# Issuing the plain copies of the weight sums on SyncE's DMA queue instead of GpSimd's

## The chip, the core and the metric

The kernel runs on one core of a Trainium2 chip. The metric is the device time of one execution in microseconds. An execution is one launch that reads all inputs from device DRAM and leaves the output there.

## What is computed

The reference is one layer of a decoder on 1024 tokens of width 1024, with 16 learned tokens put in front (T = 1040):

```
h   = concat([meta, x])                                  # (1040, 1024)
u   = rmsnorm(h, norm_mix_g)
x_lru, g_lru, v_cc, g_cc = split(u @ w_in, 4)            # 512 columns each
xc  = causal_conv(x_lru, width 4)
y_lru = rg_lru(xc) * gelu(g_lru)                         # gates, then a linear recurrence over time
c   = causal_conv(v_cc * sigmoid(g_cc), width 31)
y_cc  = silu(layernorm(c))
h   = h + concat([rmsnorm(y_lru), rmsnorm(y_cc)]) @ w_out
m   = rmsnorm(h, norm_mlp_g) @ w_mlp_up                  # 1024 -> 4096
h   = h + square(relu(m)) @ w_mlp_down                   # 4096 -> 1024
out = rmsnorm(h, norm_final_g)[16:]                      # float32
```

## The kernel before

Every large matrix product is made of three products on TensorE (PE): each float32 operand is split into a rounded part "hi" and the rest "lo", and hi*hi, hi*lo and lo*hi are added up in PSUM. A weight therefore goes through three steps: a DMA of 512 KB brings a block of 128 x 1024 numbers to SBUF, ScalarE (ACT) casts it to hi (L313), and VectorE (DVE) subtracts to get lo (L322). This is `split_w` (L556).

The tokens are worked on in two halves of 512 (the first with the 16 learned tokens). In time, the kernel does: the projection with w_in, the two convolutions and the recurrence (until about 215 us); w_out for half A (until about 270 us); the MLP of half A in 16 groups of 256 hidden columns, beside which DVE does the long convolution of half B; w_out for half B (about 540 to 580 us); and from about 680 us the MLP of half B in 8 blocks q of 512 hidden columns, by `up_fast` and `down_fast`.

`up_fast` and `down_fast` use a product scheme for 2 x 2 blocks that needs 7 block products instead of 8. Four of the seven use sums and differences of weight blocks. These depend on the weights alone, so they are made ahead of time by DMAs, into DRAM tiles `ws_up_*` and `ws_down_*`: `weight_sums` (L623) yields eight DMAs for each block, four plain copies of a weight block into t[0] to t[3], and four DMAs that add onto such a tile (`accum_op` add, L418): y onto t[0], z onto t[2], then t[0] onto t[1], then t[1] onto t[3]. There are 15 such sets (8 of up, 7 of down), 60 copies and 60 adds of 512 KB each. `load_sum` (L1176) later loads a finished sum like any weight.

The order of all instructions is set by a planner. Each step is added with a duration, what it reads and what it writes (`Plan.add`, L136); `forward` (L166) plays the steps through, engine by engine, by priority, and the program is written out in the order in which that play starts them. Its engine "sp" is SyncE, which issues DMAs alone; "pool" is GpSimd, which issues DMAs and a little arithmetic. Both issue in program order, so that an instruction which waits holds up all behind it. SyncE carries the loads of x, of w_out, w_mlp_up, w_mlp_down and of the sums, and the stores of the output (L425). GpSimd carries part of the w_in loads, small parameters, and the DMAs of the sums (`dma_pool`, L417).

The sums are spread over the plan by `tick` (L641): after every 6 us of planned PE work, from 40 us on, one DMA of a set is added, with the lowest priority and "after" that PE step. This "after" is a rule of the plan alone. In the program there is a semaphore wait only where data or a buffer demands it, or where one of the eight semaphores that a queue's DMAs use in turn is still in use.

Of the kernel before, what the change touches and what calls it, by code (L numbers as in the profile page):

```python
# [274 lines left out]
def hymba_kernel(  # L275
# [16 lines left out]
    def refs(*a):  # L292
        return [r for r in a if isinstance(r, Ref)]

    def val(v):
        return v.ap() if isinstance(v, Ref) else v
# [108 lines left out]
    def dma(o, src, nbytes, q="sp", after=()):  # L405
        e = nc.sync if q == "sp" else nc.gpsimd
        return pl.add(q, 0.47 if q == "sp" else 1.02, lambda: e.dma_start(val(o), src), [], [o],
                      nbytes=nbytes, after=after)
# [8 lines left out]
    def dma_pool(o, src, nbytes, add=False, after=()):  # L417
        kw = {"accum_op": ALU.add} if add else {}  # L418
        if add and isinstance(src, Ref):
            kw["max_dma_last_dim"] = 1024  # L420
        return pl.add("pool", 1.02, lambda: nc.gpsimd.dma_start(val(o), val(src), **kw),  # L421
                      refs(src) + ([o] if add else []), [o], nbytes=nbytes, after=after)
# [200 lines left out]
    def weight_sums(q, kind):  # L623

        blk, k, (x, y, z, v) = ((up_block, k4, ((1, 0), (1, 1), (0, 0), (0, 1))) if kind == "up"
                                else (dn_block, k2, ((0, 1), (0, 0), (1, 1), (1, 0))))
        t = [pl.fixed(dr.tile([P, 1024], F32, name=f"ws_{kind}_{q}_{n}"))[:, 0:1024] for n in range(4)]
        n = 1 << 19
        for o, src in ((t[0], x), (t[1], z), (t[2], x), (t[3], v)):
            yield lambda after, o=o, src=src: dma_pool(o.view(k), blk(q, *src), n, after=after)  # L630
        yield lambda after: dma_pool(t[0].view(k), blk(q, *y), n, True, after)
        yield lambda after: dma_pool(t[2].view(k), blk(q, *z), n, True, after)
        yield lambda after: dma_pool(t[1], t[0], n, True, after)
        wsum[q, kind] = t
        yield lambda after: dma_pool(t[3], t[1], n, True, after)

    sums = [(q, kind) for q in range(NG // 2) for kind in ("up", "down")][:-1]

    pace = {"sums": (f for s in sums for f in weight_sums(*s)), "pe": 0.0, "next": SUM_FROM}

    def tick(op):  # L641
# [130 lines left out]
    for name, src in (("a", gate_a_w), ("x", gate_x_w)):  # L772
# [3 lines left out]
            lambda a, o=o: a.rearrange("p (c n) -> p c n", c=NCT)[:, :, o * 64:(o + 1) * 64]),  # L776
# [686 lines left out]
```

## Time and profile before

| | us |
|---|---|
| three runs | 1024.51, 1024.62, 1027.83 |
| median | 1024.62 |
| the profiled execution, device time | 1022.59 |
| its span, from the first to the last instruction | 1020.8 |
| PE busy within the span | 1002.9 |
| mean granted clock of PE, as a share of the full one | 0.993 |

The rows of the profile are read like this. A row of the waits names who waited, for whom, us in total, how often, and the longest. A row of the chain of waits has the start in us, the length in us, and what ran (or which DMA was in flight). A row of the timeline has start, length, engine, line, operation, what is written <- what is read, and in brackets how long the engine stood before it and what ended that. A row of the DMA issues has the transfer, the queue that issued it, how many, KB each, and the median time in us from issue to landing. A row of the table by stretch has the stretch, its length, then busy time and number of instructions of PE, PE's weight loads, DVE, ACT and GpSimd (POOL), the granted clock as a share, the busy share of the 16 DMA engines, and GB/s. Tiles w are weights in SBUF, s and c activations, mm, tr and cv PSUM banks, ws_up and ws_down sums in DRAM.

### The profile page before, as it was taken

To read this page: it belongs to the slowest core of one execution; us is meant where nothing else is said; L and a number is where in the kernel's file an instruction comes from. 1 tells how busy PE (TensorE), PEld (TensorE's weight loads), DVE (VectorE), ACT (ScalarE), POOL (GpSimd) and SP (SyncE) were. 2 spreads that over 40 slices of the span, in tenths; PEclk is the share of its full clock that TensorE was granted. 3 is DMA by queue.
4 is the path that set the end of the run, shared out by engine and by line. 5 is a ranking of instruction groups with operands and counts; after the bars stand their busy time and mean duration, and the time that the engine had idled before them with its cause. 6 is when DMAs were issued, how large, how long until landed. Compare 5 with 4: busy or idle time off the path is not lost.

```text
span 1020.8 us, 14830 instructions
## 1 busy us (share of the span) xinstructions
PE 1002.9 (98%) x5624; PEld 864.0 (85%) x5624; DVE 833.1 (82%) x1445; ACT 524.4 (51%) x824; POOL 151.7 (15%) x179
## 2 busy tenths in 40 slices
PE   9999999999999999999899999999999999999997
PEld 7888998988797888878778888889988988989985
DVE  6798898698989999999566575577998797897875
ACT  5831045656678333334353373357666656556644
POOL 4324324212200032222222200000000000000001
PEclk9999999999999999999899999999999999999999
DMA  9449999999922299999999952234856565566522
GB/s 310 101 89 229 194 209 206 212 262 247 225 86 82 83 245 275 243 242 218 246 274 269 212 145 83 97 112 143 282 186 191 177 196 186 177 195 189 183 103 83
DMA packets 113240, 191.19 MB, mean 187 GB/s; under 512 B 6668, under 2 KB 73244, under 8 KB 113168
## 3 DMA queue, kind: packets, MB, share of 16 engines
q0 software_dynamic: 50112, 76.39, 35.4%
q1 hardware_dynamic: 63056, 113.85, 34.1%
q8 instruction: 44, 0.72, 0.3%
q14 instruction: 28, 0.23, 0.1%
HBM read 186.02 MB, written 67.11 MB: 248 GB/s over the span
## 4 chain that ended last, share of the span: by engine, by line
PE 85%; DMA 5%; DVE 4%; ACT 3%; issue 1%; SPq 0%; ACTq 0%
PE mm L388 54%; PE mm L373 17%; PE cv L373 8%; PE tr L373 4%; ACT s L315 2%; DMA s<-in_x_dram 1%; DMA w<-in_w_mlp_down_dram 1%; DVE cv L327 1%; DMA w<-in_w_mlp_up_dram 1%; DVE s L322 1%; PE tr L401 1%; DVE w L322 1%; DMA w<-in_w_out_dram 1%; ACT w L313 1%; DMA w<-in_w_in_dram 1%
## 5 line engine op out<-in xcount | busy, mean ns | idle before, releaser
L388 PE MATMUL mm<-s,w 128*128 128x512 f32 (+2 forms) x2016 | 369.5, 343 | 2.3 <-ACT w L313 1.0
L388 PEld LDWEIGHTS mm<-s,w 128*128 128x128 f32 x2016 | 315.7, 189 | 49.0 <-ACT w L313 1.3
L388 PE MATMUL mm<-w,s 128*128 128x512 f32 (+1 forms) x1260 | 299.2, 395 | 4.3 <-DVE s L322 4.3
L313 ACT CAST w<-w 128x1024 fp32r<-128x1024 f32 x193 | 200.0, 1047 | 193.1 <-DMA w<-in_w_mlp_down_dram 62.0
L388 PEld LDWEIGHTS mm<-w,s 128*128 128x128 f32 x1260 | 235.0, 189 | 59.2 <-DVE s L322 5.8
L322 DVE TENSOR_TENSOR w<-w,w 128x1024 fp32r<-128x1024 f32 x193 | 234.9, 1220 | 55.1 <-ACT w L313 54.5
L327 DVE SCALAR_TENSOR_TENSOR cv<-c,prm,cv 128x512 f32<-128x512 f32 x232 | 162.5, 750 | 0.4
L373 PEld LDWEIGHTS mm<-s,w 128*128 128x128 f32 x1152 | 139.2, 188 | 1.4
L373 PE MATMUL mm<-s,w 128*128 128x256 f32 x1152 | 140.3, 281 | 0.0
L322 DVE TENSOR_TENSOR s<-s,s 128x512 fp32r<-128x512 f32 (+4 forms) x183 | 122.3, 686 | 18.0 <-ACT s L315 15.7
L322 DVE TENSOR_TENSOR s<-mm,s 128x512 f32<-128x512 f32 x144 | 97.6, 686 | 38.5 <-PE mm L388 17.8
L315 ACT ACTIVATE s<-s 128x512 f32<-128x512 f32 (+2 forms) x152 | 95.3, 632 | 33.6 <-DVE s L322 30.7
L373 PE MATMUL cv<-w,s 128*128 128x512 f32 x336 | 83.5, 394 | 0.0
L313 ACT CAST s<-s 128x512 fp32r<-128x512 f32 (+2 forms) x83 | 50.6, 622 | 57.8 <-DVE s L322 40.1
L373 PEld LDWEIGHTS cv<-w,s 128*128 128x128 f32 x336 | 62.2, 188 | 13.7
L322 POOL TENSOR_TENSOR s<-s,s 128x512 f32<-128x512 f32 x3 | 4.6, 1541 | 421.8 <-ACT s L315 421.8
L421 POOL DMA_DIRECT2D ws_up<-in_w_mlp_up_dram x48 | 48.5, 1279 | 47.3 <-DMA ws_up<-in_w_mlp_up_dram 47.3
L313 ACT COPY s<-mm 128x512 f32<-128x512 f32 (+2 forms) x48 | 24.4, 513 | 60.2 <-PE mm L373 32.1
L421 POOL DMA_DIRECT2D ws_down<-in_w_mlp_down_dram x42 | 39.6, 1251 | 56.8 <-DMA ws_down<-in_w_mlp_down_dram 56.8
L322 DVE TENSOR_TENSOR c<-mm,c 128x512 f32<-128x512 f32 (+2 forms) x49 | 31.0, 634 | 14.4 <-PE mm L388 14.0
L315 ACT ACTIVATE s<-mm 128x512 f32<-128x512 f32 x40 | 23.7, 594 | 34.0 <-PE mm L388 33.3
L373 PE MATMUL mm<-w,s 128*128 128x512 f32 x168 | 41.1, 393 | 0.0
(133 smaller groups left out, 718.3 us busy)
## 6 DMA issues: line engine op xcount, KB each, us to landing
w<-in_w_mlp_down_dram SPq DMA_DIRECT2D x57, 512.0 KB, 4.3
w<-in_w_mlp_up_dram SPq DMA_DIRECT2D x56, 512.0 KB, 4.8
ws_up<-in_w_mlp_up_dram POOLq DMA_DIRECT2D x48, 512.0 KB, 9.4
ws_down<-in_w_mlp_down_dram POOLq DMA_DIRECT2D x42, 512.0 KB, 9.4
w<-ws_up SPq DMA_DIRECT2D x32, 512.0 KB, 3.9
w<-ws_down SPq DMA_DIRECT2D x28, 512.0 KB, 4.0
w<-in_w_in_dram POOLq DMA_DIRECT2D x24, 512.0 KB, 8.4
ws_up<-ws_up POOLq DMA_DIRECT2D x16, 512.0 KB, 7.8
```

The lines of the kernel that those rows point to most:

```text
L313: nc.scalar.copy(val(o), val(i))
L315: nc.scalar.activation(out=val(o), in_=val(i), func=func, scale=val(scale), **kw)
L322: return pl.add(eng, dur, lambda: e.tensor_tensor(out=val(o), in0=val(a), in1=val(b), op=op), refs(a, b), [o])
L327: return pl.add("dve", dur, lambda: nc.vector.scalar_tensor_tensor(out=val(o), in0=val(a), scalar=val(s), in1=val(b), op0=op0, op1=op1), r ...
L373: nc.tensor.matmul(val(p), val(a), val(b), start=start and i == 0 and k == 0, stop=k == len(pairs) - 1, skip_group_check=True)
L388: nc.tensor.matmul(val(o), val(a), val(b), start=start and k == 0, stop=stop and k == last)
L401: nc.tensor.transpose(val(o), val(i), ident.real[:rows, :rows])
L421: return pl.add("pool", 1.02, lambda: nc.gpsimd.dma_start(val(o), val(src), **kw), refs(src) + ([o] if add else []), [o], nbytes=nbytes, a ...
```

## The change

The four plain copies with which each set begins are issued by `dma` (L405), with its default queue, SyncE's, instead of `dma_pool`. The four adds of each set stay on GpSimd. The planner now counts the copies against SyncE, with 0.47 us for the issue and its rate for that queue, so some other instructions change places as well.

```
@@ -627,7 +627,7 @@
         t = [pl.fixed(dr.tile([P, 1024], F32, name=f"ws_{kind}_{q}_{n}"))[:, 0:1024] for n in range(4)]
         n = 1 << 19
         for o, src in ((t[0], x), (t[1], z), (t[2], x), (t[3], v)):
-            yield lambda after, o=o, src=src: dma_pool(o.view(k), blk(q, *src), n, after=after)
+            yield lambda after, o=o, src=src: dma(o.view(k), blk(q, *src), n, after=after)
         yield lambda after: dma_pool(t[0].view(k), blk(q, *y), n, True, after)
         yield lambda after: dma_pool(t[2].view(k), blk(q, *z), n, True, after)
         yield lambda after: dma_pool(t[1], t[0], n, True, after)
```

Three places show what moves. A row has the line, the operation, and what is written <- what is read; the last number of a tile's name is only its place in the program.

SyncE's queue at the start, between the last loads of x (s_323, s_331) and the first load of w_out:

```order
 L407 DMA s_323<-in_x_dram 128x512
 L407 DMA s_331<-in_x_dram 128x512
+L407 DMA ws_down_3_92<-in_w_mlp_down_dram 256x1x512
+L407 DMA ws_up_1_86<-in_w_mlp_up_dram 512x1x256
+L407 DMA ws_up_0_85<-in_w_mlp_up_dram 512x1x256
+L407 DMA ws_up_2_87<-in_w_mlp_up_dram 512x1x256
+L407 DMA ws_up_3_88<-in_w_mlp_up_dram 512x1x256
+L407 DMA ws_down_0_89<-in_w_mlp_down_dram 256x1x512
+L407 DMA ws_down_1_90<-in_w_mlp_down_dram 256x1x512
+L407 DMA ws_down_2_91<-in_w_mlp_down_dram 256x1x512
 L407 DMA w_1690<-in_w_out_dram 128x2x512
```

Eight copies now stand there, the first two sets; the load behind them waits for a weight buffer, they don't.

SyncE's queue in the MLP of half A, around the load that was w_4920 and is w_4919 now (issued at 478.79 us in the trace of before):

```order
+L407 DMA ws_up_0_117<-in_w_mlp_up_dram 512x1x256
 L407 DMA w_4804<-in_w_mlp_down_dram 128x1024
 L407 DMA w_4847<-in_w_mlp_down_dram 128x1024
-L407 DMA w_4920<-in_w_mlp_up_dram 128x4x256
-L407 DMA w_4927<-in_w_mlp_up_dram 128x4x256
+L407 DMA ws_up_1_118<-in_w_mlp_up_dram 512x1x256
+L407 DMA w_4919<-in_w_mlp_up_dram 128x4x256
+L407 DMA w_4926<-in_w_mlp_up_dram 128x4x256
+L407 DMA ws_up_2_119<-in_w_mlp_up_dram 512x1x256
+L407 DMA ws_up_3_120<-in_w_mlp_up_dram 512x1x256
 L407 DMA w_5048<-in_w_mlp_down_dram 128x1024
 L407 DMA w_5080<-in_w_mlp_down_dram 128x1024
```

The four copies of the set ws_up_*_117 to 120 are spread over three pairs of weight loads. GpSimd's queue at the same time, before:

```order
L421 DMA ws_up_1_126<-ws_up_0_125 512x256
L421 DMA ws_up_3_128<-ws_up_1_126 512x256
L421 DMA ws_down_0_129<-in_w_mlp_down_dram 256x1x512
L421 DMA ws_down_1_130<-in_w_mlp_down_dram 256x1x512
L421 DMA ws_down_2_131<-in_w_mlp_down_dram 256x1x512
L421 DMA ws_down_3_132<-in_w_mlp_down_dram 256x1x512
L421 DMA ws_down_0_129<-in_w_mlp_down_dram 256x1x512
L421 DMA ws_down_2_131<-in_w_mlp_down_dram 256x1x512
```

And GpSimd's queue in the changed program, the adds of the set whose copies stand in SyncE's piece above, and the first of the next set:

```order
L421 DMA ws_up_0_117<-in_w_mlp_up_dram 512x1x256
L421 DMA ws_up_2_119<-in_w_mlp_up_dram 512x1x256
L421 DMA ws_up_1_118<-ws_up_0_117 512x256
L421 DMA ws_up_3_120<-ws_up_1_118 512x256
L421 DMA ws_down_0_121<-in_w_mlp_down_dram 256x1x512
L421 DMA ws_down_2_123<-in_w_mlp_down_dram 256x1x512
```

The bunch of four copies between two sets of adds is gone; an add waits for its copy on the other queue.

SyncE's queue where half A's output is stored and half B's first `down_fast` begins, before (from 714.64 us):

```order
L407 DMA w_6903<-in_w_mlp_up_dram 128x4x256
L407 DMA w_6940<-in_w_mlp_down_dram 128x2x512
L425 DMA out_dram<-s_6938 128x512
L425 DMA out_dram<-s_6942 128x512
L425 DMA out_dram<-s_6989 128x512
L425 DMA out_dram<-s_6993 128x512
L1179 DMA w_7034<-ws_down_0_89 128x1024
L1179 DMA w_7075<-ws_down_1_90 128x1024
L425 DMA out_dram<-s_7089 128x512
```

and in the changed program:

```order
L407 DMA w_6893<-in_w_mlp_up_dram 128x4x256
L425 DMA out_dram<-s_6943 128x512
L425 DMA out_dram<-s_6947 128x512
L407 DMA w_6986<-in_w_mlp_down_dram 128x2x512
L425 DMA out_dram<-s_7000 128x512
L1179 DMA w_7030<-ws_down_0_89 128x1024
L425 DMA out_dram<-s_7002 128x512
L407 DMA ws_down_0_137<-in_w_mlp_down_dram 256x1x512
L425 DMA out_dram<-s_7045 128x512
L1179 DMA w_7079<-ws_down_1_90 128x1024
```

A copy has come in, and loads have moved behind stores, which wait for DVE: the first w_mlp_down load behind two, the load of ws_down_1 behind the first store of the next row tile.

## Rows read from the trace of the kernel before

**Rows 1.** The page: busy time of the engines, and the two DMA queues.
```profile
PE 1002.9 (98%) x5624; PEld 864.0 (85%) x5624; DVE 833.1 (82%) x1445; ACT 524.4 (51%) x824; POOL 151.7 (15%) x179
...
q0 software_dynamic: 50112, 76.39, 35.4%
q1 hardware_dynamic: 63056, 113.85, 34.1%
```

**Rows 2.** Who waited for whom, PE, in 155:166, 265:280, 430:445 and 485:500 us.
```profile
PE tr L388 <- DVE s L322: 0.8, 1, 0.8
...
PE mm L388 <- ACT s L315: 1.3, 1, 1.3
...
PE mm L388 <- DVE s L322: 0.8, 1, 0.8
...
PE mm L388 <- DVE s L322: 3.0, 1, 3.0
```

**Rows 3.** The chain of waits from 460 to 510 us.
```profile
478.79 12.81 DMA w<-in_w_mlp_up_dram
...
491.63 1.05 ACT w L313
...
492.71 1.22 DVE w L322
...
494.66 11.36 PE mm L388 x36
```

**Rows 4.** The timeline, GpSimd, just before that load.
```profile
477.10 3.20 POOL L421 DMA_DIRECT2D ws_down<-in_w_mlp_down_dram  x4
```

**Rows 5.** The chain of waits, its other weight loads before 478 us.
```profile
141.32 6.56 DMA w<-in_w_out_dram
...
265.58 6.71 DMA w<-in_w_mlp_down_dram
...
423.68 7.53 DMA w<-in_w_mlp_down_dram
```

**Rows 6.** DMA issues from 360 to 500 us (two rows) and 610 to 680 us.
```profile
ws_down<-in_w_mlp_down_dram POOLq DMA_DIRECT2D x18, 512.0 KB, 9.4
w<-in_w_mlp_up_dram SPq DMA_DIRECT2D x12, 512.0 KB, 7.3
...
w<-in_w_mlp_up_dram SPq DMA_DIRECT2D x5, 512.0 KB, 3.7
```

**Rows 7.** Busy time by stretch, with clock and DMA share behind POOL's time.
```profile
360.00:590.00 230.00, 226.18 (x1004) 182.32 (x1003) 184.25 (x300) 84.39 (x119) 58.97 (x65) 0.99 0.99 246
...
493.80:500.70 6.90, 6.04 (x14) 4.78 (x15) 6.69 (x21) 1.04 (x1) 1.06 (x1) 0.51 0.84 138
...
715.00:745.00 30.00, 30.00 (x214) 28.04 (x213) 30.00 (x67) 22.05 (x35) 0.00 (x0) 1.00 0.79 266
```

**Rows 8.** The timeline from 22 to 62 us, four of its rows.
```profile
23.41 0.33 SPq L407 DMA_DIRECT2D s<-in_x_dram  x1
...
29.84 1.69 POOL L407 DMA_DIRECT2D w<-in_w_in_dram  x2 [0.88 <-DVE c L322]
...
37.48 0.67 ACT L313 CAST gw_x_hi<-s 128x512 fp32r<-128x512 f32 x1
...
43.29 1.06 ACT L315 ACTIVATE w<-w 128x1024 fp32r<-128x1024 f32 x1
```

**Rows 9.** DMA issues from 24 to 31 us.
```profile
w<-in_w_in_dram POOLq DMA_DIRECT2D x2, 512.0 KB, 5.1
...
s<-in_lru_gate_x_w_dram POOLq DMA_DIRECT2D x2, 64.0 KB, 3.1
```

**Rows 10.** The timeline, SyncE's queue, from 680 to 800 us.
```profile
726.46 0.34 SPq L425 DMA_DIRECT2D out_dram<-s  x1
...
782.74 0.38 SPq L407 DMA_DIRECT2D w<-in_w_mlp_up_dram  x1
```

**Rows 11.** The timeline, PE, from 725 to 745 us.
```profile
740.57 2.94 PE L373 MATMUL cv<-w,s 128*128 128x512 f32 x12
```

More of the change, by code (lines that the diff above doesn't have):

```diff
@@ L629, in weight_sums @@
         for o, src in ((t[0], x), (t[1], z), (t[2], x), (t[3], v)):
-            yield lambda after, o=o, src=src: dma_pool(o.view(k), blk(q, *src), n, after=after)
+            yield lambda after, o=o, src=src: dma(o.view(k), blk(q, *src), n, after=after)
         yield lambda after: dma_pool(t[0].view(k), blk(q, *y), n, True, after)
```

## The prediction, made before the changed kernel was run

> **What bounds the kernel now.** I read the page first, then who waited for whom on PE, then the chain of waits, then the DMA issues. PE is busy 1002.9 of 1020.8 us [rows 1], so no change of queues can bring more than the 17.9 us in which PE stands, and the matmul time while the clock is low. Start and end of the kernel hold about half of the 17.9 us; in between lie four stalls that end on DVE or ACT: 0.8, 1.3, 0.8 and 3.0 us [rows 2].
>
> The chain shows what is behind the largest. A weight load issued at 478.79 took 12.81 us to land; the ACT cast of that weight starts the moment it lands, the DVE subtraction follows, and PE goes on at 494.66 [rows 3]. The weight itself was not urgent. ACT and DVE work in program order: while the cast waits, DVE's evacuation of a PSUM bank stands behind the subtraction, and PE has no bank. Just before the load, GpSimd had issued four plain copies at 477.10 [rows 4]. The other three stalls have a late weight load in the chain too: 6.56, 6.71 and 7.53 us [rows 5]. Where nothing of GpSimd is in flight, the same load lands in 3.7 us (610 to 680); between 360 and 500 us it takes 7.3 us and the copies beside it 9.4 us [rows 6]. From 360 to 590 us the 16 DMA engines are busy 0.99 of the time [rows 7].
>
> The 3.0 us stall costs more than itself. From 493.8 to 500.7 the granted clock is 0.51, the lower of the two levels, right after PE stood, and PE is busy 6.04 us there [rows 7]. At the upper level that work takes half, so the low clock costs another 3.0 us.
>
> **What the change does.** It removes 60 plain copies of 512 KB from GpSimd and puts them on SyncE; the 60 adding DMAs and all bytes stay. First the price of a copy, for which no row exists on SyncE's queue. The GpSimd queue moved 76.39 MB in 35.4% of 1020.8 us, which is 2.5 us of all 16 engines per 512 KB; SyncE's queue moved 113.85 MB in 34.1%, which is 1.6 us [rows 1]. A copy on SyncE lies between 1.6 and 2.5 us. I take 2.5 us, since GpSimd's figure holds mostly DMAs that write to DRAM, as a copy does. Its issue is one more SyncE instruction (0.4 us), on an engine that mostly waits for buffers: nothing.
>
> What moves is the moment. The planner's PE pacing of the sums is not a wait in the program: on GpSimd the copies ran in bunches of four as soon as the adds ahead of them had landed. On SyncE a copy stands behind weight loads that wait for a buffer which PE frees, so the copies are now spread at PE's pace, up to about 783 us [rows 10], and each set of four adds on GpSimd has to wait for its copies. Three places:
>
> The middle, 360 to 500 us. By the order printed above, one copy leaves with the load pair ahead of the load of 478.79, and two leave behind that load and its neighbour. GpSimd then stands at the set of ws_up_0_117, whose second add needs a copy that comes after that load. So around 479 us there is no bunch of four copies, and at most one add. The load should land in 4 to 7 us, not 12.8 [rows 6]. At 7.3 us, the median of that stretch, the cast would start at 486 instead of 491.6, 5.5 us earlier, against a stall of 3.0: it goes, and with it the low clock, 6.0 us in all. At 423.68 and 265.58 the copies ahead leave with earlier load pairs too; these loads need to win 0.8 and 1.3 us, and the distance to 3.7 us is 3.8 and 3.0 us [rows 2, 5, 6]. At 141.32 GpSimd has adds and w_in loads as before, but no copies; I take that 0.8 as well. Sum: 6.0 + 0.8 + 1.3 + 0.8 = 8.9 us; at least 0, if DMAs that move instead land beside the same loads. What is late next in the middle is DVE, which had idle time behind these casts; I see no second stall hidden within the gain, but where one is, it takes a part of it.
>
> The start. Eight copies are now issued on SyncE right behind the last x loads, from about 24 us [rows 8], which is 13 to 20 us of DMA time. Beside them GpSimd's gate loads of 64 KB land in 3.1 us and are cast at 37.48, and two w_in loads issued at 29.84 land in 5.1 us, with ACT's operation on the first at 43.29 [rows 8, 9]. If the two queues share evenly, the w_in loads (3.2 us of engine time) take some 4 to 7 us more and still land before 43; the gate loads, out by 29, may take twice as long. If GpSimd's queue got nothing until the copies are through (about 45 us), ACT would be 5 us late or more, and PE with it, since ACT's work feeds the matmuls there. I take 0: with both queues loaded, at 360 to 500, GpSimd's DMAs did land in 9.4 us [rows 6].
>
> The end of the sums, 715 to 745 us. Here GpSimd was silent, the DMA engines are busy 0.79, DVE is busy 30.00 of 30.00 us and PE as well [rows 7]. The change puts four copies and about two adds into it: 23.7 us plus 11 to 15 us of DMA work in 30 us, an excess of 5 to 9 us. By the order, the load of ws_down_1, which stood ahead of the store that came at 726.46, now stands behind it [rows 10]. Issued at 726.9 and landing in 4 to 7 us, plus a cast of 1.05 and a subtraction of 1.22 us [rows 3], it is ready at 733 to 736; its product ran at 740.57 [rows 11]. That is 4 to 7 us of room against an excess that grows to 5 to 9. From 0 to 5 us of stall; I take 2. A stall of 3 us would bring the low clock back, another 3 us.
>
> Sum: -8.9 + 2 = -6.9 us. The profiled execution took 1022.59 us, 2.0 under the median of the runs, 1024.62, so I carry the difference over: 1015.7 for such an execution, 1018 us for the median.
>
> **Two rules weighed against the trace.** A load lands in 3.7 us alone and in 12.81 beside the bunch [rows 3, 6], a factor of 3.5. The Trainium skill, page "DMA: Bandwidth & Descriptors", section "Queues, rings and completion order", says that each DMA engine goes round between the queues that have work, a packet from each. By that rule a load shares with GpSimd's queue at worst half and half, about 7.4 us however much GpSimd has queued, and a copy in the load's own queue is the worse neighbour, because the load stands behind the whole of it. The trace does not bear out the half; that SyncE's own queue keeps its order, no run here shows yet. It is the ground for rival 3. The same page, section "Issuing engines are not separate DMA queues", says that DMAs of all issuers run on the same 16 engines, so that another issuer saves only issue time: by it the sum is 0, which is rival 1.
>
> **The rivals.**
> 1. Nothing but the queue's name changes: the DMA work is the same, 60 copies and 60 adds, and late loads turn up at other casts as often. For it: the bytes and the engines are the same. Against it: the four stalls lie in stretches where the DMA engines are full, and there are half-empty ones to move into. Time 1024.6, between 1021 and 1028.
> 2. The middle gains its 8.9 us and the stretch from 715 to 785 us gives most of it back: a stall of 4 to 5 us there and the low clock's 3 us. Decided by whether loads land later than some 9 us there. 1022 to 1025.
> 3. Slower: the copy ahead in SyncE's own queue costs a load what GpSimd's bunch did. In the new order five loads follow a copy that is issued less than 1 us ahead (w_2036, w_4488, w_5329, w_6532, w_7146). If such a load lands in 13 us, as one copy's 9.4 and its own 3.7 [rows 6], it is a second case of 478.79, at 6.0 us each, and the gain in the middle is lost. With one or two of the five at an urgent cast: 1024.6 + 6 to 12, about 1033. It decides from a landing of about 10 us; against it speaks that the copy occupies the engines 2.5 us, not 9.4.
> That copies come too late for their sums is excluded by room: the last set's last copy stands 54 SyncE DMAs ahead of the first load of its sums.
>
> **How the numbers follow.** Forecast (1014 to 1021): 0.53. Rival 1: 0.17. Rival 2: 0.15. Rival 3: 0.15. About 0.5% (5 us) is what a measurement of this kernel can tell from no change, so faster means below 1019.5 and slower above 1029.7. Of the forecast 0.48 lies below 1019.5, and 0.01 of rival 2; rival 3 has 0.13 above 1029.7, rival 1 and 2 together 0.02. So 0.49 faster, 0.36 same, 0.15 slower. For 8 in 10 the range leaves out 0.04 below 1013 and most of rival 3 above 1029. The forecast's own range is 1014 to 1021.
>
> **What would show it.** Right: between 360 and 590 us the DMA share falls to 0.6 to 0.8, w_mlp_up loads land in about 5 us, PE's waits for DVE lose the 3.0 us one, no low clock near 494, GpSimd's DMAs reach to about 800 us. Rival 1: the waits on PE keep their sum at other times. Rival 2: a PE wait of 3 us or more between 715 and 785, with a low clock behind it. Rival 3: loads of 10 us or more behind copies in the chain of waits. At the start: an ACT wait for w_in before 50 us would be the case I set at 0. The prediction is wrong if PE's waits in the middle remain although the bunches are gone.

## The result, and the profile after

Five runs of the changed kernel took 1013.03 to 1014.70 us, median 1014.32; five of the kernel before, beside them, 1024.51 to 1027.83, median 1024.78. The ratio is 0.9885, with a 95% interval from 0.9868 to 0.9903: 10.5 us less, where 6.6 were forecast (1018 from 1024.62). The profiled execution took 1014.32 us, its span is 1012.5 us.

The page of the changed kernel, against [rows 1] (queues: packets, MB, share of 16 engines):

```profile
PE 997.9 (99%) x5624; PEld 860.9 (85%) x5624; DVE 831.9 (82%) x1445; ACT 524.3 (52%) x824; POOL 106.4 (11%) x119
...
q1 hardware_dynamic: 87568, 145.31, 42.9%
q0 software_dynamic: 41472, 44.93, 27.5%
```

31.5 MB moved from one queue to the other. As time of all 16 engines, GpSimd's queue fell from 361 us (35.4% of 1020.8) to 278, SyncE's rose from 348 to 434: 83 us off one, 86 onto the other, so a copy costs 1.4 us of the engines on either. The DMA work is the same, 710 and 713 us in all. What changed is who waits. All of PE's waits from 50 us to its last matmul, against the four of [rows 2]:

```profile
PE mm L388 <- DVE s L322: 1.3, 2, 0.8
PE cv L373 <- DVE w L322: 0.6, 1, 0.6
```

The stalls at 160, 273, 441 and 491 us are gone. Two small ones are new, 0.8 at 398.7 and 0.6 at 760.4; a 0.5 at 326 was there before (at 329). By stretch, the three of [rows 7] (stretch, length, busy time and instructions of PE, weight loads, DVE, ACT, POOL, then clock, DMA share, GB/s):

```profile
360.00:590.00 230.00, 229.14 (x1032) 185.20 (x1031) 187.02 (x306) 92.20 (x135) 22.70 (x22) 1.00 0.75 192
493.80:500.70 6.90, 6.90 (x35) 5.71 (x34) 1.38 (x2) 4.63 (x6) 0.51 (x1) 1.00 0.73 161
715.00:745.00 30.00, 30.00 (x178) 26.45 (x177) 29.88 (x50) 18.10 (x26) 3.13 (x3) 1.00 1.07 345
```

The DMA share of the middle fell from 0.99 to 0.75, PE's clock near 494 from 0.51 to 1.00, and the DMA work turned up at 715 to 745 us, where the engines are now full (1.07; a packet is counted whole where it starts, so a share can pass 1) and PE is busy 30.00 of 30.00 us all the same.

At the place of the load of 478.79 [rows 3, 4], the timeline has on SyncE's queue

```profile
475.81 2.94 SPq L407 DMA_DIRECT2D w<-in_w_mlp_up_dram  x2
478.80 1.23 SPq L407 DMA_DIRECT2D ws_up<-in_w_mlp_up_dram  x2
```

and on GpSimd's, in brackets how long it had stood:

```profile
461.57 1.18 POOL L421 DMA_DIRECT2D ws_up<-in_w_mlp_up_dram  x1 [14.82 <-DMA ws_up<-in_w_mlp_up_dram]
483.95 1.15 POOL L421 DMA_DIRECT2D ws_up<-in_w_mlp_up_dram  x1 [21.21 <-DMA ws_up<-in_w_mlp_up_dram]
```

The load pair leaves first, its copies right behind it, and GpSimd stands 21.21 us for a copy. The pair's first load, the one of 478.79 in the kernel before, landed in 3.7 us instead of 12.8 (DMA issues from 475.5 to 477 us):

```profile
w<-in_w_mlp_up_dram SPq DMA_DIRECT2D x1, 512.0 KB, 3.7
```

The DMA issues from 360 to 500 us, against [rows 6] (queue, count, KB, median us to landing):

```profile
w<-in_w_mlp_up_dram SPq DMA_DIRECT2D x12, 512.0 KB, 3.9
...
ws_up<-in_w_mlp_up_dram SPq DMA_DIRECT2D x8, 512.0 KB, 5.8
```

7.3 us became 3.9, and the copies themselves land in 5.8 to 6.3 us instead of 9.4.

Laid side by side, matmul by matmul (by the names of their tiles PE runs them in the same order in both, but for 18 of them between 690 and 729 us), the changed kernel is 0.1 us ahead at 98 us, 3.2 at 271, 9.0 from 492 to 690, and 7.8 from 765 us on.

### The profile page after: what moved, and what is told of

Its sections match the earlier page's. It is cut to its first block, busy times and chain, and to the rows that moved or that the text cites. A ratio compares the mean times of both kernels' runs of the same rounds, so it can differ in the third digit from the quotient of the medians.

```text
span 1012.5 us, 14840 instructions
## 1 busy us (share of the span) xinstructions
PE 997.9 (99%) x5624; PEld 860.9 (85%) x5624; DVE 831.9 (82%) x1445; ACT 524.3 (52%) x824; POOL 106.4 (11%) x119
## 4 chain that ended last, share of the span: by engine, by line
PE 89%; DVE 4%; ACT 3%; DMA 2%; issue 1%; SPq 1%; ACTq 0%; DVEq 0%
PE mm L388 58%; PE mm L373 17%; PE cv L373 8%; PE tr L373 4%; DMA w<-in_w_in_dram 2%; ACT s L315 2%; DVE s L322 1%; PE tr L401 1%; DVE cv L327 1%; DVE w L322 1%; SPq L407 1%; PE tr L388 1%; PE cv L401 1%; ACT L315 1%; ACT w L313 0%
## 5 line engine op out<-in xcount | busy, mean ns | idle before, releaser
L388 PEld LDWEIGHTS mm<-w,s 128*128 128x128 f32 x1260 | 233.7, 188 | 54.5 <-DVE s L322 1.9
L373 PEld LDWEIGHTS cv<-w,s 128*128 128x128 f32 x336 | 62.2, 188 | 14.4 <-DVE w L322 0.9
L313 ACT COPY s<-mm 128x512 f32<-128x512 f32 (+2 forms) x48 | 24.4, 514 | 71.8 <-PE mm L373 36.4
L421 POOL DMA_DIRECT2D ws_up<-in_w_mlp_up_dram x16 | 18.8, 1212 | 216.4 <-DMA ws_up<-in_w_mlp_up_dram 204.5
L421 POOL DMA_DIRECT2D ws_down<-in_w_mlp_down_dram x14 | 15.4, 1177 | 217.9 <-DMA ws_down<-in_w_mlp_down_dram 217.9
L373 PEld LDWEIGHTS mm<-w,s 128*128 128x128 f32 x168 | 31.6, 188 | 7.3
```

What stands on the lines that cost most here:

```text
L313: nc.scalar.copy(val(o), val(i))
L373: nc.tensor.matmul(val(p), val(a), val(b), start=start and i == 0 and k == 0, stop=k == len(pairs) - 1, skip_group_check=True)
L388: nc.tensor.matmul(val(o), val(a), val(b), start=start and k == 0, stop=stop and k == last)
```

## The experiments

Where a ratio is given, it is to runs of the kernel before on the same chip; those had medians of 1026.9 (e1 to e4), 1025.8 (e5 to e8) and 1026.7 us (e9 to e12).

**The theory at the outset**: the gain comes from when the copies move, not from what they cost. On GpSimd they leave in bunches of four, at any moment. The two **rivals**: the queue itself (copies are cheaper or share better on SyncE's); and the planner, which put other steps in another order, most of them from about 640 us on. In e1, e4, e9, e11 and e12 PE, ACT and DVE run exactly the changed kernel's order, in e2, e5 and e8 exactly that of before. Where stalls are read below, they are those of the one profiled execution, which need not be a typical one.

### Plan and queue apart (e1, e2)

e1 keeps the changed kernel's plan and issues the copies by GpSimd:

```
-            yield lambda after, o=o, src=src: dma(o.view(k), blk(q, *src), n, after=after)
+            yield lambda after, o=o, src=src: pl.add("sp", 0.47, lambda: nc.gpsimd.dma_start(
+                o.view(k).ap(), blk(q, *src)), [], [o], nbytes=n, after=after)
```

> The planner's order of PE, ACT and DVE is that of the changed kernel, but the 60 copies are issued by GpSimd again, each at the place in time that the plan gave it on SyncE. Theory (the gain comes from when the copies move: on GpSimd they stand behind adds that wait, and leave in bunches of four): the bunches are back, a late weight load holds ACT and DVE at one to three places, and the time is 1021 to 1026 us. Rival, the planner's other order of the steps from 640 us on made the gain: 1013 to 1016 us.

Measured: 1029.2 us, ratio 1.0018 (0.9997 to 1.0039). Its chain of waits has two late weight loads before 290 us:

```profile
231.14 19.76 DMA w<-in_w_mlp_up_dram
...
270.95 8.79 DMA w<-in_w_mlp_down_dram
```

Beside the first, the timeline has a bunch of GpSimd's:

```profile
229.63 3.35 POOL L630 DMA_DIRECT2D ws_down<-in_w_mlp_down_dram  x4
```

The second left as the last copy of the next bunch landed, beside two adds (266.29 and 269.41). PE waits from 245 to 290 us for what stands behind the casts of these loads:

```profile
PE mm L388 <- ACT s L315: 3.5, 2, 3.4
PE tr L388 <- ACT s L313: 2.0, 1, 2.0
```

The same plan is worth nothing with the copies on GpSimd. e2 is the other half: the plan of before, copies issued by SyncE.

```
-            yield lambda after, o=o, src=src: dma_pool(o.view(k), blk(q, *src), n, after=after)
+            yield lambda after, o=o, src=src: pl.add("pool", 1.02, lambda: nc.sync.dma_start(
+                o.view(k).ap(), blk(q, *src)), [], [o], nbytes=n, after=after)
```

> The planner's order is that of the kernel before (copies planned against GpSimd), but the copies are issued by SyncE. Theory (when the copies move): SyncE's weight loads, which wait for buffers, spread the copies, and the time is 1013 to 1018 us. Rival, the planner's other order: 1022 to 1026 us.

Measured: 1021.4 us, ratio 0.9940 (0.9915 to 0.9965), between the two. The middle is as quiet as expected (from 400 to 530 us PE waits 0.4 us in all), but there is one new stall. PE's longest wait from 715 to 745 us:

```profile
PE cv L373 <- DVE c L322: 6.1, 1, 6.1
```

The chain of waits behind it:

```profile
719.80 0.34 SPq L425
...
720.19 0.55 SPq L630
...
720.84 12.59 DMA w<-in_w_mlp_down_dram
```

And the granted clock behind the stall:

```profile
738.30:745.10 6.80, 4.96 (x12) 3.92 (x13) 6.53 (x9) 4.50 (x6) 2.08 (x2) 0.50 1.01 267
```

A store waits for DVE until 719.80; the copy (L630) and the load behind it on SyncE then leave together, beside an add that GpSimd issues at 719.92. The load lands after 12.59 us. (This execution took 1024.24 us, 2.8 over the median of e2, so the stall need not be as long in the others.) This is rival 2 of the prediction with its place and its low clock, in a kernel in which only the plan differs. In the changed kernel the load of the same row left at 716.21, ahead of a copy, and landed in 6.6 us.

### The excess at 715 to 745 us (e8)

e2, with one set's copies back on GpSimd:

```
+            e = nc.gpsimd if (q, kind) == (6, "down") else nc.sync
+            yield lambda after, o=o, src=src, e=e: pl.add("pool", 1.02, lambda: e.dma_start(
+                o.view(k).ap(), blk(q, *src)), [], [o], nbytes=n, after=after)
```

> As e2 (plan of before, copies issued by SyncE), but the four copies of the set ws_down_137 to 140 are issued by GpSimd, which puts them at about 690 us instead of 714 to 734. In e2 PE stood 6.05 us at 734 for a w_down load that landed after 12.6 us, with 6.8 us of low clock behind it. Theory (the copies are the excess of DMA work at 715 to 745 us that delays this load): the stall goes, 1012 to 1016 us. Rival (SyncE stands at a store that waits for DVE at 719.8, and the loads behind it are late whatever the copies do): a stall of 3 us or more stays there, 1018 to 1022 us.

Measured: 1017.3 us, ratio 0.9926 (0.9900 to 0.9951). PE's waits from 690 to 745 us:

```profile
PE mm L388 <- DVE ty L336: 1.4, 1, 1.4
PE mm L373 <- ACT s L313: 0.9, 1, 0.9
PE cv L373 <- DVE c L322: 0.6, 1, 0.6
```

The 6.1 is a 0.6 and the low clock at 738 is gone, though the store and the loads behind it stand in the same order; the load behind the store now lands in 5.6 us. So the copies make the load late, not the store alone. The time is 1 us above what was expected, because the bunch, now on GpSimd at 687 to 689 us, makes a load there late (12.3 us) and with it two new stalls, 1.4 and 0.9 us. By the ratios e8 and e2 can't be told apart; the profile at this place is what tells them.

### The bunch, and the queue (e3, e4, e6)

e3 leaves all copies on GpSimd and changes their order inside a set, so that the adds' waits pace them:

```
...
+        yield copy(t[0], x)
         yield lambda after: dma_pool(t[0].view(k), blk(q, *y), n, True, after)
+        yield copy(t[2], x)
         yield lambda after: dma_pool(t[2].view(k), blk(q, *z), n, True, after)
+        yield copy(t[1], z)
         yield lambda after: dma_pool(t[1], t[0], n, True, after)
+        yield copy(t[3], v)
...
```

> All copies stay on GpSimd; inside each set a copy now stands right ahead of the add that needs it (copy, add, copy, add, ...), so that the adds' waits pace the copies and never four are in flight. Theory (when the copies move, whatever queue issues them): no PE stall of 3 us near 490, no low clock in the middle, 1013 to 1018 us. Rival, the queue itself (GpSimd's copies cost more engine time, 2.5 against 1.6 us, or share worse with the loads): the middle keeps late loads, 1021 to 1026 us.

Measured: 1021.1 us, ratio 0.9944 (0.9915 to 0.9974): half of the gain, and neither expectation. From 400 to 530 us PE waits 1.4 us instead of 3.8, the stall at 491 is gone. But at 160 us there is a stall of 3.0 us with a low clock behind it (in an execution of 1025.86 us, 4.8 over the median of e3); the chain shows a load issued half a microsecond after GpSimd's add and two copies (143.82 to 145.03):

```profile
145.57 10.60 DMA w<-in_w_out_dram
```

So without bunches late loads cost less, by the time, but they are not gone. e4 has the plan of the changed kernel with `nc.scalar.dma_start` in the place of `nc.gpsimd.dma_start` in e1's edit:

> The plan of the changed kernel, but the copies are issued on ScalarE's queue, a third one. Theory (when the copies move): ACT's program order spreads them at the pace of ACT's work, so again no bunch; the 60 issues cost ACT some us of its idle time; 1013 to 1018 us. Rival, a copy must stand in the weight loads' own queue so as not to compete with them (order within the queue is what helps): loads beside a copy land in 7 us or more as before, 1019 to 1026 us.

Measured: 1014.55 us, ratio 0.9879 (0.9848 to 0.9910), as the changed kernel, with one stall of 2.4 us at 691 that the changed kernel lacks (in an execution of 1018.28 us, 3.7 over the median of e4). The rival, that a copy must stand in the loads' own queue, falls. That GpSimd's queue costs nothing by itself is not shown: copies on GpSimd that wait for a load pair were not tried. e6 goes the other way: SyncE's queue, but four copies at once.

```
...
+        def copies(after):
+            for o, src in ((t[0], x), (t[1], z), (t[2], x), (t[3], v)):
+                dma(o.view(k), blk(q, *src), n, after=after)
+        yield copies
+        for _ in range(3):
+            yield lambda after: None
```

> As the changed kernel, but the four copies of a set are handed to SyncE together, so that loads stand right behind bunches of four in their own queue. Theory (a bunch that is in flight beside a load is what costs, on either queue): a load behind four copies lands in 10 us or more, one to three casts are late, 1017 to 1025 us. Rival (only GpSimd's bunches cost, since copies on SyncE's queue take 1.6 us of the engines): 1013 to 1016 us.

Measured: 1016.4 us, ratio 0.9917 (0.9892 to 0.9941). Here my theory of the bunch fell: sixty copies in fifteen bunches, and from 100 to 600 us PE waits 0.5 us in all (what it has over the changed kernel are waits of 3.1 us from 680 to 750). The timeline of SyncE's queue shows why:

```profile
405.33 0.93 SPq L407 DMA_DIRECT2D w<-in_w_mlp_up_dram  x2
406.31 2.53 SPq L407 DMA_DIRECT2D ws_down<-in_w_mlp_down_dram  x4
418.80 1.04 SPq L407 DMA_DIRECT2D w<-in_w_mlp_down_dram  x2
```

The bunch leaves the moment the load pair ahead of it has left, and the next loads wait until 418.80 for buffers that PE frees. The four copies have landed by 417.3. So the number of copies in flight is not what counts, but that they leave with no load close behind them that is wanted soon. (Some loads do stand close behind a bunch: those of 515.33 and 518.52 us land in 10.0 and 10.6, and PE does not wait for them.)

### Ahead of a load, or behind one (e10)

The second theory: SyncE's program order ties the copies to the rhythm of the loads, and puts them behind a load pair, where there are some 10 us without a load. e10 is e6 with the bunches one place earlier on SyncE (all but those of the first two sets and of the last three), most of them between the two loads of a pair. PE, ACT, DVE and GpSimd run the same instructions in the same order as in e6 (the line numbers are 12 higher):

```
...
+        out = sorted(self.ops, key=lambda o: (start[o.seq], o.seq))
+        last, group = None, []
+        for o in list(out):
+            if o.eng != "sp":
+                continue
+            if o.seq in self.copies:
+                if last is not None:
+                    out.remove(o)
+                    out.insert(out.index(last), o)
+            else:
+                last = o if start[o.seq] > 45 and "dma.<locals>" in o.fn.__qualname__ else None
+        return out
...
```

> As e6 (the four copies of a set handed to SyncE together), but every bunch stands one place earlier: ahead of the load that it stood behind, that is between the two loads of a pair. Copies, adds, bytes, queue and the order of the other engines are those of e6. Theory (what counts is whether a copy is in flight ahead of a load that ACT soon wants): the second load of such a pair lands in 8 us or more instead of 4.6, several casts are late, 1019 to 1027 us. Rival (copies on SyncE's queue are cheap wherever they stand): 1015 to 1018 us as e6.

Measured: 1024.3 us, ratio 0.9986 (0.9961 to 1.0010). One place in one queue took back 7 to 8 us, nearly the whole gain of e6. The timeline at 370 us:

```profile
370.15 0.38 SPq L419 DMA_DIRECT2D w<-in_w_mlp_up_dram  x1
370.58 2.59 SPq L419 DMA_DIRECT2D ws_up<-in_w_mlp_up_dram  x4
373.27 0.81 SPq L419 DMA_DIRECT2D w<-in_w_mlp_up_dram  x1
```

That last load, by the DMA issues at 373.27:

```profile
w<-in_w_mlp_up_dram SPq DMA_DIRECT2D x1, 512.0 KB, 11.7
```

One step of what was expected is wrong: not several casts stall PE, but few. From 200 to 600 us the second loads of such pairs land in 8.6 to 11.7 us, and PE waits 0.5 us; a late load costs only where its cast is wanted before it lands. It is so in the projection with w_out, where the chain has

```profile
145.54 11.92 DMA w<-in_w_out_dram
```

and PE's waits from 150 to 170 us are

```profile
PE tr L400 <- ACT s L325: 4.3, 1, 4.3
```

with the lower clock behind it:

```profile
163.20:170.00 6.80, 5.23 (x17) 4.50 (x18) 6.09 (x13) 2.83 (x6) 1.03 (x1) 0.50 0.98 145
```

PE's 5.23 us of work there would take 2.6 at the upper level, so this one load costs about 7 us, most of what e10 lost in this profile. At 690 to 755 us five waits add up to 4.3 us, where e6 has 3.1.

### Which sets, and where (e9, e12)

e9 has the changed kernel's plan, with the six sets of blocks 3 to 5 alone on SyncE.

```
+            e = nc.sync if q in (3, 4, 5) else nc.gpsimd
...
```

> The plan of the changed kernel, but only the copies of the six sets of blocks 3 to 5 (those that ran between about 257 and 508 us) are issued by SyncE, the others by GpSimd as in e1. Theory by the terms of the prediction (6.8 of its 8.9 us lie at 441 and 491): the stalls from 400 to 525 us go, those at 160 and at 250 to 280 stay, 1016 to 1022 us. Rival (the sets before 257 us count for more than the prediction gave them): 1022 to 1027 us, with stalls of 5 us and a low clock before 285 us.

Measured: 1032.6 us, ratio 1.0063 (1.0036 to 1.0089), outside both. The middle did what the theory said: from 290 to 600 us PE waits 0.7 us. But the sets on SyncE are paced by PE, so the sets behind them come later, and on GpSimd they now leave at

```profile
676.91 3.20 POOL L631 DMA_DIRECT2D ws_down<-in_w_mlp_down_dram  x4
...
706.62 3.42 POOL L631 DMA_DIRECT2D ws_up<-in_w_mlp_up_dram  x4
```

in the MLP of half B, whose chain then has

```profile
685.83 13.20 DMA w<-in_w_mlp_up_dram
...
721.00 10.47 DMA w<-in_w_mlp_down_dram
```

and PE waits there

```profile
PE mm L373 <- ACT s L313: 7.5, 2, 4.2
```

In the kernel before GpSimd was through by about 591 us and no bunch met half B's loads. So this part of the change is worse than none of it. e12 undoes the start: the first two sets on GpSimd (`q > 0` in the same line).

> The plan of the changed kernel, but the eight copies of the first two sets, which the changed kernel issues at 25 to 33 us on SyncE, are issued by GpSimd. Theory (the start is worth nothing, as the prediction put it): 1013 to 1016 us, and the loads of gate weights and w_in beside the start land in 3 and 5 us again instead of 6 and 10 to 13. Rival (the copies at the start cost, or save, some us there, since the clock's low stretch at 36 us is missing in the changed kernel's profile): more than 2 us off the changed kernel either way.

Measured: 1015.0 us, ratio 0.9894 (0.9858 to 0.9930): the start can't be told from nothing. The DMA issues from 24 to 31 us in the changed kernel, against [rows 9]:

```profile
w<-in_w_in_dram POOLq DMA_DIRECT2D x2, 512.0 KB, 11.3
```

and in e12:

```profile
w<-in_w_in_dram POOLq DMA_DIRECT2D x2, 512.0 KB, 4.8
```

The eight copies do hold up these loads by 6.5 us. They land at 39.44 and 42.95 in the changed kernel; ACT's operation on the first starts at 43.15, and the next of its kind at 46.95. Of the room, 3.7 us are left.

### The kernel before again, and the floor (e5, e7)

> The kernel before, unchanged, to see a second profiled execution of it beside the first. The time is that of before, 1023 to 1028 us. Theory: the bunches of copies make late loads in every execution, but not at the same casts, so that an execution has two to five stalls and 6 to 14 us of stall and low clock in the middle; the profiled one of 1022.59 us was one with few. Rival: the same four stalls stand in the second profile, at the same casts and sizes, and the 2 us between the first profile and the median lie outside the kernel's body.

Measured: 1026.2 us, ratio 1.0005 (0.9977 to 1.0032): by the time no difference. The program is that of before, but its second profile, of an execution of 1026.94 us, has other stalls than [rows 2]. PE's waits from 400 to 530 us are

```profile
PE mm L388 <- DVE s L322: 4.3, 3, 1.5
PE mm L388 <- ACT s L315: 0.4, 1, 0.4
```

at 423, 448 and 499 us, with full clock near 494; at 276 it waits 2.2 us with a low clock behind it. Its chain has

```profile
230.49 17.27 DMA w<-in_w_mlp_up_dram
```

PE stood 14.4 us in this execution and 10.4 in the first. The timeline of GpSimd at that moment, the end of one set, the four copies of the next and an add of it:

```profile
227.48 1.02 POOL L421 DMA_DIRECT2D ws_up<-ws_up  x1 [7.76 <-DMA ws_up<-ws_up]
228.11 3.20 POOL L421 DMA_DIRECT2D ws_down<-in_w_mlp_down_dram  x4
236.21 1.09 POOL L421 DMA_DIRECT2D ws_down<-in_w_mlp_down_dram  x1 [4.89 <-DMA ws_down<-in_w_mlp_down_dram]
```

Seventeen runs of the kernel before, beside e5, went from 1019.3 to 1034.8 us; those of e11 and e12, both near the changed kernel, from 1012.9 to 1016.1.

e7 leaves out the copies and the adds, and `load_sum` reads a plain weight block (PE and DVE run in the order of the kernel before).

> The floor: the copies and the adds of the weight sums are left out, and the loads of sums read a plain weight block of the same size instead (so the MLP of half B is computed from other weights). Theory (copies and adds cost time only by late loads): what is left in the changed kernel is two stalls of 0.8 and 0.6 us, so 1010 to 1014 us. Rival (the DMA traffic beside them still slows all loads in the changed kernel, or GpSimd's adds cost elsewhere): under 1008 us.

Measured: 1011.0 us, ratio 0.9865 (0.9835 to 0.9895). PE's waits after 50 us:

```profile
PE mm L388 <- DVE s L322: 0.5, 1, 0.5
```

and its GpSimd queue moves only what is left beside the sums:

```profile
q0 software_dynamic: 13376, 13.47, 7.0%
```

So the sums cost the kernel before about 14 us, and the changed kernel about 2 by its own ratio, with 3 us of uncertainty. e11 tries for the rest: the two loads of norm_final_g on SyncE too (`"sp"` for `"pool"` in that call).

> The changed kernel with the two loads of norm_final_g (256 KB each, about 383 us) on SyncE's queue too. In the changed kernel two w_mlp_up loads landed after 11 to 12 us beside them, and PE stood 0.8 us at 398.7. Theory: that stall goes, 1012.5 to 1014 us, the difference hardly above what the runs scatter. Rival (the two adds beside those loads make the stall): it stays, 1014 to 1015 us.

Measured: 1013.6 us, ratio 0.9881 (0.9846 to 0.9917). The stall at 398.7 us is gone, as expected, and the time can't be told from the changed kernel's. I found no version that beats it by more than the runs scatter.

## Why the prediction was right in kind and wrong in size

**What bounded the kernel: right.** The late weight load, the cast that waits, the work that stands behind it, PE that waits for that work: e1, e2 and e9 each show it at another place. In e1 and e9 that work is ACT's own (`PE <- ACT s`), not DVE's evacuation. One reading was off: PE's waits behind 50 us add up to 6.7 of the 17.9 us, so start and end hold 11.2, rather more than half.

**The middle, -8.9: right, with luck in the sum.** By the matmuls side by side the lead grows by 8.9 us between 98 and 492 us. The terms are not quite the forecast's: the waits of [rows 2] with the 0.3 beside the first add up to 6.2 us; they went, and the low clock's 3.0 us or a little more with them, and the new stall at 398.7, which the prediction did not have, takes 0.8 back. That loads land sooner holds: in 3.9 us where I took 4 to 7. But the reason it gave, no bunch beside the loads, is only half of it. e6 has bunches and from 100 to 600 us no stall that the changed kernel lacks, e3 has none and a stall of 3.0 at 160. The position behind a load pair decides (e10).

**The copy's price: too high.** The bounds were 1.6 and 2.5 us, taken 2.5; the two queues' totals give 1.4 on either, below both. GpSimd's mean was high because of the adds: without the sums its queue takes 71 us (7.0% of e7's span), with the 60 adds 278, so an add costs 3.5 us.

**715 to 745 us, +2 (0 to 5): the first step that failed.** The stretch did fill up, from 0.79 to 1.07, some 8 us of engine time against the 11 to 15 worked out. PE did not wait there: the lead is 8.7 us at 745 instead of 9.0, so the term measured 0.3 us and not 2. The prediction called the room 4 to 7 us and the excess 5 to 9; the loads landed in 5.1 to 12.7 us, and ACT waited for none of them from 715 to 762 us. The room was misread too: the load of ws_down_1, which it put at 726.9, behind a store, left at 715.27, with a store earlier than thought, and landed in 5.1 us. The 0.6 at 760, with which the lead falls to 7.8, is not the copies' either: it stands before the same matmul, 0.57 or 0.58 us long, in all six executions of the changed order (also in e1, with the copies on GpSimd) and in none of another, and no load is in the chain before it. It is a price of the planner's order. That this hangs on the order, e2 shows: there the same copies cost 6.1 us and a low clock when one load stands behind a store and a copy. Such a term turns on two or three instructions in SyncE's queue, and the right forecast was one of two cases, not a mean between them.

**The 2.0 us between the profiled execution and the median: the second step that failed.** I carried it over as a constant. The changed kernel's profiled execution is its median, and e5 shows what such a difference is made of: its profiled execution is 4.4 us longer than the first, and PE stood 4.0 us more, in more of the same stalls, at other casts. I count the 2.0 to what the change takes away; the executions at the median were not traced. Profile against profile the kernel gained 8.3 us where 6.9 were forecast; the other 2.2 of the 10.5 are this, and more than half of the 3.9 us by which the forecast fell short.

**The start, 0: right.** The loads of w_in are 6.5 us later and still 3.7 us ahead of ACT. PE's stall at 20.5 us grew from 1.0 to 2.5, before any copy is issued (the first leaves at 25.51), and that at 35 from 0.7 to 1.0; the low clock of 36.4 to 39.9, which cost before 1.7 us, is missing. The two cancel (0.1 us at 98), which is luck as far as the copies go: e12, without copies there, has a stall of 1.7 at 21 us and no low clock either.

**The rivals.** Rival 1, only the name changes: the bytes and the engine time did stay, and the time did not. The Trainium skill, page "DMA: Bandwidth & Descriptors", section "Issuing engines are not separate DMA queues", says that starting DMAs from several engines at once saves only the time that a sequencer takes to start them. By the DMA engines' work that agrees (710 and 713 us); the kernel's time it does not tell, as e1 and the changed kernel differ by 1.3% with the issuer alone. The issuer's program order sets when a DMA starts. Rival 2: it did not come in the changed kernel, but in e2. Rival 3: the five loads right behind a copy landed in 5.8 to 9.1 us and none stalled PE. Its price was nearly right (e10: 8.6 to 11.9 us behind four copies), its threshold of 10 us was not, since most casts in the middle have more room.

That a load loses more than half its rate beside GpSimd's queue, which the prediction read from one row, holds in two more: 17.27 and 19.76 us in e5 and e1. Both are the second load of a pair; with nothing of GpSimd's in flight such a load landed in 4.6 us (e6, 405.80). By the round between queues that the Trainium skill, page "DMA: Bandwidth & Descriptors", section "Queues, rings and completion order", describes, an estimate is a factor of two at most. The traces do not agree: 17.27 is 3.8 times 4.6. In e5 the four copies, the pair's two loads and, whole or in part, three adds (about two by their time) were in flight. By the prices below and 1.6 us for a load (348 us of SyncE's queue for 113.85 MB) that is an estimate of 16 us of the engines: the load landed about as late as if it had been served last. The kernel before has a like case at 230 us, where a load that left 0.05 us ahead of a bunch landed in 5.5 us and its neighbour, 0.46 us later, in 12.2. How the engines share between the queues was not tried and stays open.

## What to carry to other kernels

Put background DMAs on a queue whose program order already follows the loads' rhythm (SyncE's here, or ACT's, which does the casts), and behind loads, not close ahead of them: there they fall into the time in which the loads wait for buffers. When you move only a part, look where the rest ends up: in e9 the sets left on a free-running queue slid to a place where they hurt more, in e12 two sets left at the start cost nothing that could be told. And where a profile's stalls come from chance meetings, as here, the distance between the profiled execution and the median can be made of the same stalls, and go with them.

## What was not expected of the hardware

- A copy from DRAM to DRAM of 512 KB takes 1.4 us of all 16 DMA engines whether SyncE or GpSimd issues it; an adding DMA of the same size takes 3.5 us (both from the queues' totals, before, after and e7).
- A weight load of 512 KB, the second of a pair, that lands in 4.6 us with nothing of GpSimd's in flight (e6) took 17.27 and 19.76 us beside a bunch of GpSimd's and its adds (e5, e1).
- Three of the five runs of the changed kernel had a mean clock of 0.998 and took 1014.3 to 1014.7 us; the other two had 0.996, so more time at the low level, and took 1013.0 and 1013.4. A lower mean clock was not the longer run here.
